# Gated DeltaNet block loop: other slots for a block's last pieces, another bank for the outputs, another way of the inverses to their rows

## The chip, the cores and the metric

The kernel runs on one core of one Trainium2 chip. The metric is the device time of one execution, in microseconds (us). The time of the kernel before is 2538.49 us, the median of three runs (2527.29 to 2549.32).

## The reference, cut to what matters

One inference step of a hybrid encoder layer: 4096 tokens of a prompt and 32 of a running stream, each token 1024 wide. Group A is a short gated convolution, group B a gated delta rule with 4 heads of 128. The change lies in group B and where group B meets group A.

```python
h    = rmsnorm(x, ln_pre);  proj = h @ w_in         # split into B_a C_a X_a Z_a | qkv | Z_g | decay, beta
y_a  = B_a * conv3(C_a * X_a) * silu(Z_a)           # group A
q, k, v = silu(conv4(qkv));  q, k = l2norm(q), l2norm(k)      # group B, per chunk of 64 tokens and head:
a_mat = tril(kbeta @ k^T * decay, -1)
t_mat = solve_triangular(I + a_mat, I)              # the inverses that the change carries in another way
u, w  = t_mat @ (v * beta), t_mat @ (kbeta * exp(g))
v_new = u - w @ S;  o = (q * exp(g)) @ S + (q @ k^T * decay) @ v_new
S     = S * exp(g_last) + k_dec^T @ v_new           # from chunk to chunk, 64 chunks in a row
y_g   = rmsnorm_head(o) * silu(Z_g)
y     = x + rmsnorm_post(concat(y_a, y_g) @ w_out)
```

In the kernel a chunk is 128 tokens (4 rows of 32 per inverse, merged to 128).

## The kernel before, in words

**Blocks and slots.** Group B goes over 16 prompt blocks of 256 tokens (two chunks each; the 32 sample tokens go along with block 0). A block runs eight pairs of projections (`steps`: k, k, q, q, v, v, z, z). A pair is two runs of 24 matmuls of 128x256 on TensorE (PE), and behind each run there is a *slot*: block gi has slots s0 = 16*gi to s0 + 15. What is not a projection is cut into pieces, which `at_slot` puts into a numbered slot and `run_slot` runs there. With `T.on` set, PE keeps exactly the order in which its matmuls are written; the other engines are ordered by a scheduler from what depends on what.

**A block's own pieces.** Slots s0 + 7 to s0 + 12: norms of q and k, Gram matrices (`gram`, tiles `gt`, `kd`, `at`), then `subst`. Slots s0 + 2 to 13 also hold the next block's gates and its normalized input. `subst` inverts 32x32 triangles by forward substitution on GpSimd (POOL): one scaling of `la` (L547, 128x1024), then 31 steps of two operations (L551, L552) on `lt`. In the kernel before, `lt` is stored in DRAM (L555, tile `ltd`) and read back by eight DMAs of 32-byte runs (L562) into `Tc`.

**A block's last pieces** run during the next block and a half (`finish`, slots from s0 + 22 on). `rec_a` of chunk c is four pieces: `rt` (transposed v); `rk`, `rq` (products with the state S); `rv` (inverse times right side, copied by ScalarE (ACT) to `vn`, L652); `rS` (new state, L659). `merge` is five pieces: it transposes `Tc` to `U` on VectorE (DVE, L583), and makes the 128x128 inverses from the 32x32 ones by small matmuls into a bank of PSUM called "m", with VectorE's `Rx` (L599) and ACT's copies to U (L605) between. `rec_b` is two pieces: `oo` (inner part of the output, bank "o", L670 ff.), then norms on VectorE and ACT (L682) and `om` (transposed output, bank "o" too), which VectorE multiplies into the gate `zg` (L688), and a DMA stores `zg` (L693). A bank that two pieces share makes the second wait until the first has been read.

**Queues.** All DMAs named here are issued by SyncE (SP) in order; they take eight counters in turn, so that one waits until the DMA eight before it has landed. Weight columns of group A are prepared during blocks 1 to 13 (`prep_a`; its first step on VectorE is L206, behind a load from DRAM); blocks 4, 7 and 10 begin two such columns.

**After block 15** the pieces that are left run one after the other with no projections between them; then group A begins (`operands`, `a_sample`, `a_pairs`), whose products are sums of 12 matmuls of 128x256 by a Strassen-Winograd scheme (`winograd`).

The pieces of a block's end stand in the code as:

```python
at_slot(s0 + 28, next, ra[1])        # rt of chunk 1
at_slot(s0 + 34, ends, rb[0])        # om of chunk 0
at_slot(s0 + 35, ends, ra[1])        # rS of chunk 1
at_slot(s0 + 35, next, rb[1])        # oo of chunk 1
at_slot(s0 + 39, ends, rb[1])        # om of chunk 1
```

Of the kernel before, what the change touches and what calls it, by code (L numbers as in the profile page):

```python
# [18 lines left out]
P = 128  # L19
# [30 lines left out]
def hybrid_kernel(  # L50
# [471 lines left out]
    def subst(b):  # L522
# [30 lines left out]
        b["subst_end"] = getattr(last, "ins", last)  # L553
        ltd = dp.tile([4, 32, 256], F32, tag="ltd", bufs=2, name=f"ltd{b['id']}")
# [13 lines left out]
    def merge(b):  # L568
# [11 lines left out]
        Tf = Tc.rearrange("p c h e -> p (c h) e")  # L580
        for q in range(nb):
            s = slice(32 * q, 32 * q + 32)
            V.transpose(Uf[s, :, s], Tf[s])  # L583
# [11 lines left out]
        for q in (0, 2):  # L595
            s0, s1 = slice(32 * q, 32 * q + 32), slice(32 * q + 32, 32 * q + 64)
            for c, h in ch:
                T.matmul(px[s1, c, h], M[c][s0, h, s1], Tc[s0, c, h], start=True, stop=True)
            V.tensor_tensor(X[s1], px[s1], bc(nb_[s1], 3, 32), ALU.mult)  # L599
# [63 lines left out]
    def rec_b(b, c):  # L663
# [5 lines left out]
        po = bank("o", [P, NH, P], f"o{nm}")[:C]  # L669
# [154 lines left out]
    def finish(p, s0):  # L824
# [5 lines left out]
        if n == 1:  # L830
            for i, g in enumerate((ra[0], ra[0], mg, ra[0], ra[0], rb[0])):
                at_slot(s0 + 16 + i, next, g, None)
            at_slot(s0 + 24, ends, rb[0])
            at_slot(s0 + 24, out_state, p)
            return
        at_slot(s0 + 22, next, ra[0])
        at_slot(s0 + 23, next, ra[0])
        for i in range(5):
            at_slot(s0 + 24 + i, next, mg, None)
        at_slot(s0 + 29, next, ra[0])  # L840
        at_slot(s0 + 30, ends, ra[0])
        at_slot(s0 + 30, next, rb[0])
        at_slot(s0 + 28, next, ra[1])
        at_slot(s0 + 32, next, ra[1])
        at_slot(s0 + 34, next, ra[1])
        at_slot(s0 + 34, ends, rb[0])
        at_slot(s0 + 35, ends, ra[1])
        at_slot(s0 + 35, next, rb[1])
        at_slot(s0 + 39, ends, rb[1])
        if p["last"]:  # L850
            at_slot(s0 + 36, out_state, p)
# [83 lines left out]
    T.on = False  # L935
    early.close()
    for i in sorted(slots):
        run_slot(i)
    late.close()
# [3 lines left out]
    pl2 = ctx.enter_context(tc.tile_pool(name="pl2", bufs=1, side="right", reuse_waits="tile"))  # L943
# [32 lines left out]
    def winograd(lts, rhs, ps, c11, c12, c21, c22):  # L976
# [4 lines left out]
        for i, p in enumerate(ps):  # L981
            mm3(p, lts[i], rhs[i], True, True)
            if i == 0:
# [154 lines left out]
    rm = t3([P, KT], F32, "rm")  # L1138

# [151 lines left out]
    a_pairs(1, ops[1], 0)  # L1291
    for i in range(4, 8):
# [67 lines left out]
```

## Time and profile before

| | us |
|---|---|
| median of three runs | 2538.49 |
| lowest, highest | 2527.29, 2549.32 |
| the profiled execution's own time | 2536.03 |
| its span | 2534.2 |
| blocks 1 to 14 and what is left of 0 (236.57 to 1413.73) | 1177.16 |
| PE, DVE, ACT, POOL busy in the whole span | 2178.5, 1697.0, 1003.4, 1168.1 |

The profile is one execution. Rows of a timeline read: start, duration, engine, line, operation, output tile <- input tiles, shape, how many in a row, and in brackets how long the engine had been idle before it and on what. PEclk is the granted TensorE clock as a share of 2.4 GHz; 0.50 is the lower level, 1.2 GHz. Tile names are those of the code without buffer numbers. An engine's idle time costs something only where another engine waits for it.

### The profile page before, as it was taken

The numbers are of one execution on the slowest core, as the hardware profiler recorded it, in microseconds if no ns is written. First come the engines' busy times: TensorE is split into PE (matmuls) and PEld (weight loads), VectorE is DVE, ScalarE is ACT, GpSimd is POOL, SyncE is SP. The second block draws the span as 40 slices with busy tenths as digits, with TensorE's granted clock in tenths as the row PEclk, the third lists the DMA queues.
The fourth block names the chain that finished last, engine by engine and source line by source line (L and its number), as shares of the span: only waits on it lengthen the run. The fifth ranks groups of instructions, "written<-read, shape, count | busy, mean of one in ns | idle before, by whom it ended". The sixth has DMA issues, their size and how long they took to land. (4 is left out here: it accounts for less than half of the span.)

```text
span 2534.2 us, 48623 instructions
## 1 busy us (share of the span) xinstructions
PE 2178.5 (86%) x18626; PEld 1745.3 (69%) x18626; DVE 1697.0 (67%) x4666; ACT 1003.4 (40%) x2497; POOL 1168.1 (46%) x1581
## 2 busy tenths in 40 slices
PE   4666988699878987888889879999999999999998
PEld 3555776577767776777777768878888888544443
DVE  4885767676777677767865667556667466576772
ACT  4453555355545554555554422112221111333331
POOL 3524532544454445344642464175665442265552
PEclk9777988898999888989989889999999999999999
DMA  6343323423332433234422331521212103344331
GB/s 117 53 106 78 80 60 72 89 69 101 80 90 63 108 79 90 62 102 86 92 55 52 114 104 27 202 76 49 77 51 75 51 30 134 111 146 153 115 128 67
DMA packets 296914, 221.40 MB, mean 87 GB/s; under 512 B 166392, under 2 KB 236856, under 8 KB 296680
## 3 DMA queue, kind: packets, MB, share of 16 engines
q1 hardware_dynamic: 296680, 218.28, 31.4%
q8 instruction: 146, 2.39, 0.4%
q14 instruction: 88, 0.72, 0.1%
HBM read 127.84 MB, written 74.64 MB: 80 GB/s over the span
## 5 line engine op out<-in xcount | busy, mean ns | idle before, releaser
L74 PEld LDWEIGHTS <-w 128*128 128x128 f16 x6528 | 640.8, 103 | 126.0 <-POOL w L714 24.2
L74 PE MATMUL pj_c<-hhi,w 128*128 128x256 f16 x3072 | 583.3, 290 | 0.0
L74 PE MATMUL pj_c<-hlo,w 128*128 128x256 f16 x1536 | 445.4, 290 | 0.0
L74 PEld LDWEIGHTS <-w_a 128*128 128x128 f16 x2880 | 272.1, 99 | 62.2 <-issue 26.5
L547 POOL TENSOR_TENSOR la<-la,lt 128x1024 f32<-128x1024 f32 x16 | 37.8, 2361 | 581.7 <-DVE lt L542 536.7
L74 PEld LDWEIGHTS <-opm 128*128 128x128 f16 x1536 | 149.1, 98 | 189.3 <-issue 13.8
L552 POOL TENSOR_TENSOR lt<-lt 128x112 f32<-128x112 f32 (+29 forms) x496 | 237.5, 479 | 38.7
L551 POOL TENSOR_TENSOR lt<-la,lt 128x112 f32<-128x112 f32 (+29 forms) x496 | 219.0, 442 | 38.9
L436 DVE SCALAR_TENSOR_TENSOR qk<-u,cw,qk 128x256 f32<-128x256 f32 x384 | 208.4, 587 | 4.8 <-ACT qk L434 4.8
L74 PE MATMUL pja<-op,w_a 128*128 128x256 f16 x1536 | 193.8, 276 | 6.7 <-ACT d L984 2.7
L74 PE MATMUL pj_z<-hhi,w 128*128 128x256 f16 x1024 | 180.3, 275 | 0.0
L74 PE MATMUL ga<-op,w_a 128*128 128x256 f16 x1152 | 152.2, 279 | 14.6 <-DVE w L988 7.0
L1186 POOL TENSOR_TENSOR mab<-mab 128x1024 bf16<-128x1024 bf16 (+2 forms) x48 | 103.6, 2158 | 128.1 <-ACT mab L1184 125.7
L74 PE MATMUL pj_z<-hlo,w 128*128 128x256 f16 x512 | 140.5, 274 | 0.0
L74 PE MATMUL pjo<-w_o,opm 128*128 128x512 f16 x528 | 118.2, 379 | 3.8 <-DVE v13y L1261 2.0
L74 PE MATMUL ro<-w_o,opm 128*128 128x512 f16 x504 | 113.1, 379 | 4.3 <-DVE v7y L1261 2.3
L988 DVE TENSOR_TENSOR w<-pja,w 128x256 f32<-128x256 f32 x168 | 67.3, 420 | 73.7 <-PE pja L74 70.6
L74 PE MATMUL go<-w_o,opm 128*128 128x512 f16 x504 | 112.7, 379 | 3.9 <-DVE v19y L1261 2.0
L1003 ACT ACTIVATE op<-tsc 128x512 f16<-128x512 f32 x60 | 37.8, 630 | 192.9 <-POOL tsc L1009 113.0
L468 ACT ACTIVATE jk<-gt 128x128 bf16<-128x128 f32 x256 | 71.0, 278 | 100.8 <-PE gt L77 95.2
L988 DVE TENSOR_TENSOR w<-ga,w 128x256 f32<-128x256 f32 x121 | 51.0, 422 | 77.6 <-PE ga L74 69.8
L436 DVE SCALAR_TENSOR_TENSOR v<-u,cw,v 128x256 f32<-128x256 f32 x192 | 84.6, 477 | 9.0 <-ACT v L434 9.0
(697 smaller groups left out, 4664.0 us busy)
## 6 DMA issues: line engine op xcount, KB each, us to landing
xt<-in_x_prompt_dram SPq DMA_DIRECT2D x32, 512.0 KB
op<-hTd SPq DMA_DIRECT2D x32, 512.0 KB
mx<-mxd SPq DMA_DIRECT2D x16, 1024.0 KB
xtw<-in_w_in_dram SPq DMA_DIRECT2D x28, 512.0 KB
wad<-hl SPq DMA_DIRECT2D x56, 256.0 KB
gB<-gd SPq DMA_DIRECT2D x16, 516.0 KB
hTd<-hhi SPq DMA_DIRECT2D x16, 512.0 KB
hTd<-hlo SPq DMA_DIRECT2D x16, 512.0 KB
```

Source lines behind the costliest of these rows:

```text
L74: return self.queue(nc.tensor.matmul(*a, **k))
L436: V.scalar_tensor_tensor(d, u[:, i, j:j + n], cw[:, j, c0 + i:c0 + i + 1], d, ALU.mult, ALU.add)
L468: A.activation(jk[:C], tp[:C, h, :], AF.Square, accum_out=b["ss"][:, c, x, h:h + 1])
L547: E.tensor_tensor(la, la, bc(rl, 1, 32), ALU.mult)
L551: E.tensor_tensor(tm, bc(la[:, j, j + 1:32], 2, w), bc(lt[:, j, 0:w], 1, r), ALU.mult)
L552: last = E.tensor_tensor(lt[:, j + 1:32, 0:w], lt[:, j + 1:32, 0:w], tm, ALU.subtract)
L988: V.tensor_tensor(dst, p, src, ALU.add)
L1003: A.activation(f[:, q, 0, hf], t, AF.Copy)
L1186: G.tensor_tensor(ab[:, 0:m], ab[:, 0:m], ab[:, m:2 * m], ALU.add)
```

## The change

1. **Inverses to rows.** `subst` no longer stores `lt` in DRAM. One VectorE transpose of 32x32 blocks writes `lt` into the first 256 columns of `la`, and 16 DMAs from SBUF to SBUF (32 rows of 256 bytes each) bring them to `Tc`, which now has the layout [P, 4, 2, NH, 8]. The transposes to U and the merge's first matmuls read that layout with another access pattern. The sample's path stays.
2. **Slots.** A block's last pieces start two slots later and end five slots later, with at most one piece of a chunk's chain in a slot in most places.
3. **Bank.** `rec_b`'s `po` goes to bank "m" (so its tile reads `mo` instead of `oo`).
4. **The end.** The pieces left after block 15 run between the products of group A's first two column blocks (`a_pairs(0, ., 0)` and `a_pairs(1, ., 0)`), behind each second product of `winograd`; the pools opened after them, and `operands(4)` to `(7)`, stand behind that.

```diff
--- before.py
+++ after.py
@@ -551,6 +551,16 @@
             E.tensor_tensor(tm, bc(la[:, j, j + 1:32], 2, w), bc(lt[:, j, 0:w], 1, r), ALU.mult)
             last = E.tensor_tensor(lt[:, j + 1:32, 0:w], lt[:, j + 1:32, 0:w], tm, ALU.subtract)
         b["subst_end"] = getattr(last, "ins", last)
+        if not b["s"]:
+
+            X = la.rearrange("p a b -> p (a b)")[:, 0:256].rearrange("p (q m e) -> p q m e", q=4, e=8)
+            V.transpose(X.rearrange("p q m e -> p e m q"), lt.rearrange("p a e -> p e a"))
+            Tc = b["Tc"] = tl([P, 4, 2, NH, 8], F32, "Tc", 1, b["id"])
+            for q in range(4):
+                for g in range(4):
+                    dma(Tc[32 * q:32 * q + 32, g].rearrange("p c h e -> p (c h e)"),
+                        X[32 * g:32 * g + 32, q].rearrange("p m e -> p (m e)"))
+            return
         ltd = dp.tile([4, 32, 256], F32, tag="ltd", bufs=2, name=f"ltd{b['id']}")
         dma(ltd.rearrange("g l f -> (g l) f"), lt.rearrange("p a b -> p (a b)"))
         tcl = te([P, 1, NH, 32], F32, "Tcs", 1, "s") if b["s"] else tl([P, 2, NH, 32], F32, "Tc", 1, b["id"])
@@ -577,10 +587,10 @@
         U = U2
         b["U"] = [U[:, c] for c in range(2)]
         Uf = U.rearrange("p c h e -> p (c h) e")
-        Tf = Tc.rearrange("p c h e -> p (c h) e")
+        Tf = Tc.rearrange("p g c h e -> p (c h) g e")
         for q in range(nb):
             s = slice(32 * q, 32 * q + 32)
-            V.transpose(Uf[s, :, s], Tf[s])
+            V.transpose(Uf[s, :, s].rearrange("p a (g e) -> p a g e", e=8), Tf[s])
         nm = b["id"]
         ch = [(c, h) for c in range(2) for h in range(NH)]
 
@@ -595,7 +605,8 @@
         for q in (0, 2):
             s0, s1 = slice(32 * q, 32 * q + 32), slice(32 * q + 32, 32 * q + 64)
             for c, h in ch:
-                T.matmul(px[s1, c, h], M[c][s0, h, s1], Tc[s0, c, h], start=True, stop=True)
+                T.matmul(px[s1, c, h].rearrange("p (g e) -> p g e", e=8), M[c][s0, h, s1], Tc[s0, :, c, h],
+                         start=True, stop=True)
             V.tensor_tensor(X[s1], px[s1], bc(nb_[s1], 3, 32), ALU.mult)
         yield
         for q in (0, 2):
@@ -666,7 +677,7 @@
         nm = f"{b['id']}_{c}"
         sl = slice(c * C, (c + 1) * C)
         o, vn = b["rec"].pop(c)
-        po = bank("o", [P, NH, P], f"o{nm}")[:C]
+        po = bank("m", [P, NH, P], f"o{nm}")[:C]
         for h in range(NH):
             T.matmul(po[:, h], b["at"][c][:, h, :C], vn[:, h], start=True, stop=True)
         V.tensor_tensor(o, o, po, ALU.add)
@@ -828,27 +839,17 @@
         rb = [rec_b(p, c) for c in range(n)]
         mg = merge(p)
         if n == 1:
-            for i, g in enumerate((ra[0], ra[0], mg, ra[0], ra[0], rb[0])):
-                at_slot(s0 + 16 + i, next, g, None)
-            at_slot(s0 + 24, ends, rb[0])
-            at_slot(s0 + 24, out_state, p)
+            for i, g in ((19, ra[0]), (20, ra[0]), (23, mg), (24, ra[0]), (25, ra[0]), (25, rb[0])):
+                at_slot(s0 + i, next, g, None)
+            at_slot(s0 + 30, ends, rb[0])
+            at_slot(s0 + 30, out_state, p)
             return
-        at_slot(s0 + 22, next, ra[0])
-        at_slot(s0 + 23, next, ra[0])
-        for i in range(5):
-            at_slot(s0 + 24 + i, next, mg, None)
-        at_slot(s0 + 29, next, ra[0])
-        at_slot(s0 + 30, ends, ra[0])
-        at_slot(s0 + 30, next, rb[0])
-        at_slot(s0 + 28, next, ra[1])
-        at_slot(s0 + 32, next, ra[1])
-        at_slot(s0 + 34, next, ra[1])
-        at_slot(s0 + 34, ends, rb[0])
-        at_slot(s0 + 35, ends, ra[1])
-        at_slot(s0 + 35, next, rb[1])
-        at_slot(s0 + 39, ends, rb[1])
+        for i, g in ((24, ra[0]), (25, ra[0]), (26, mg), (27, mg), (28, mg), (29, mg), (30, mg), (30, ra[1]),
+                     (31, ra[0]), (33, ra[0]), (33, rb[0]), (35, ra[1]), (37, ra[1]), (38, rb[0]),
+                     (39, ra[1]), (39, rb[1]), (44, rb[1])):
+            at_slot(s0 + i, next, g, None)
         if p["last"]:
-            at_slot(s0 + 36, out_state, p)
+            at_slot(s0 + 40, out_state, p)
 
     def first_group(grp):
 
@@ -932,15 +933,11 @@
             if b["last"]:
                 out_hist(b)
         prevs = grp
-    T.on = False
     early.close()
-    for i in sorted(slots):
-        run_slot(i)
-    late.close()
 
 
     pe2 = ctx.enter_context(tc.tile_pool(name="pe2", bufs=1, side="left", reuse_waits="tile"))
-    pl2 = ctx.enter_context(tc.tile_pool(name="pl2", bufs=1, side="right", reuse_waits="tile"))
+    pl2 = None
 
     def t2(shape, dtype, tag, bufs=1, nm=""):
         return pe2.tile(shape, dtype, tag=tag, bufs=bufs, name=f"{tag}{nm}")
@@ -980,6 +977,8 @@
 
         for i, p in enumerate(ps):
             mm3(p, lts[i], rhs[i], True, True)
+            if i % 2 and slots:
+                run_slot(min(slots))
             if i == 0:
                 A.activation(c21, p, AF.Copy)
             else:
@@ -1135,8 +1134,6 @@
         V.tensor_copy(hr, hp)
         dma(dst[0, 0].rearrange("j (c p) -> (j c) p", p=P), hr)
 
-    rm = t3([P, KT], F32, "rm")
-
     def prep_out(i):
 
         w = t3([P, 2, D], F32, "mx", 2, f"w{i}")
@@ -1289,6 +1286,12 @@
     a_sample(0)
     a_pairs(0, ops[0], 0)
     a_pairs(1, ops[1], 0)
+    while slots:
+        run_slot(min(slots))
+    T.on = False
+    late.close()
+    pl2 = ctx.enter_context(tc.tile_pool(name="pl2", bufs=1, side="right", reuse_waits="tile"))
+    rm = t3([P, KT], F32, "rm")
     for i in range(4, 8):
         operands(i)
     a_pairs(0, ops[0], 1)
```

**PE, last pieces of block 6, which run in block 7.** In a row stand the line, the operation, output <- inputs, shape; `pj_c` is a projection, `rv_1`, `rS_1` and `oo_1` belong to chunk 1, `om_0` to chunk 0. Before, ahead of the run of 24 projections between `rv` and `rS`:

```order
L74 MATMUL pj_c_10863<-hhi_9848,w_22_507 128x256
L74 MATMUL rv_1_10888<-R_1_10476,U 128x128 x4
L77 MATMUL om_0_10895<-ident,o_0_10109 128x128 x4
L74 LDWEIGHTS w_23_510
L74 MATMUL pj_c_10863<-hhi_9848,w_23_510 128x256
```

and behind that run of 24:

```order
L74 MATMUL pj_c_10863<-hhi_9848,w_23_511 128x256
L74 MATMUL rS_1_10972<-vn_1_10893,kd_1_9149 128x128 x4
L74 MATMUL oo_1_10982<-vn_1_10893,at_1_9424 128x128 x4
L74 LDWEIGHTS w_16_681
L74 MATMUL pj_c_11008<-hhi_9848,w_16_681 128x256
```

Now `rv` stands two runs of 24 ahead of `rS`, and `om_0` one run ahead of it. The end of the second run and what follows:

```order
L74 MATMUL pj_c_11090<-hhi_9871,w_18_857 128x256
L77 MATMUL om_0_11115<-ident,o_0_10276 128x128 x4
L74 LDWEIGHTS w_19_860
L74 MATMUL pj_c_11090<-hhi_9871,w_19_860 128x256
```

```order
L74 MATMUL pj_c_11090<-hhi_9871,w_19_861 128x256
L74 MATMUL rS_1_11159<-vn_1_11088,kd_1_9148 128x128 x4
L74 MATMUL mo_1_11169<-vn_1_11088,at_1_9445 128x128 x4
L77 MATMUL gt_0_11196<-ident,qk_10803 128x128 x4
L74 LDWEIGHTS w_24_1208
```

What moved: a whole run of projections lies between `rv` and `om_0` and another between `om_0` and `rS`; `rS` and the output product still stand side by side, but the latter is in the merge's bank.

**VectorE in block 7, around the second q pair** (`u_2`, `qk`: that pair's convolution; `o`, `so`, `S`: last pieces of the block before). Before:

```order
L688 SCALAR_TENSOR_TENSOR zg_7586<-om_1_10088,gwc,zg_7586 128x4x128
L431 COPY hist_9725<-u_2_10075 128x6
L436 SCALAR_TENSOR_TENSOR qk_9722<-u_2_10075,cw,qk_9722 128x256
L639 SCALAR_TENSOR_TENSOR R_0_10046<-rk_0_10095,sm_9453,R_0_10046 128x128 x4
L436 SCALAR_TENSOR_TENSOR qk_9722<-u_2_10075,cw,qk_9722 128x256 x5
L471 TENSOR_TENSOR kd_0_10124<-gt_0_10115,E_9602 128x512
L429 COPY u_10_10389<-hist_8640 128x2x3
L583 STREAM_TRANSPOSE U<-Tc_9538 32x8x32 x4
L599 TENSOR_TENSOR Rx_10187<-m_10188,sm_9453 32x256 x2
```

Now:

```order
L699 SCALAR_TENSOR_TENSOR zg_7592<-om_0_10054,gwc,zg_7592 128x4x128
L557 STREAM_TRANSPOSE la_9480<-lt_9481 128x8x8x4
L431 COPY hist_9745<-u_2_10085 128x6
L670 SCALAR_TENSOR_TENSOR S_1_10103<-S_0_9815,E_7484,rS_1_10098 128x128 x4
L436 SCALAR_TENSOR_TENSOR qk_9742<-u_2_10085,cw,qk_9742 128x256 x2
L683 TENSOR_TENSOR o_1_9955<-o_1_9955,mo_1_10108 128x512
L436 SCALAR_TENSOR_TENSOR qk_9742<-u_2_10085,cw,qk_9742 128x256 x2
L471 TENSOR_TENSOR kd_0_10144<-gt_0_10135,E_9632 128x512
L593 STREAM_TRANSPOSE U<-Tc_9558 32x8x32
L436 SCALAR_TENSOR_TENSOR qk_9742<-u_2_10085,cw,qk_9742 128x256 x2
L689 TENSOR_TENSOR so_1_10114<-so_1_10114,sm_8382 128x4
```

What moved: a new transpose out of `lt` stands right ahead of the q pair's copy, and the four transposes to U no longer stand together; the other three follow 6, 17 and 27 rows behind the first. Counted one by one, 11, 17, 28 and 41 instructions stand between the new transpose and the four.

**SP in block 7, around the DMAs of the inverses.** Before, and now:

```order
L555 DMA ltd_9536<-lt_9460 128x256
L736 DMA wad_122<-hl_0_10126 128x1024
L562 DMA Tc_9538<-ltd_9536 128x4x8 x8
L693 DMA mxd_112<-zg_7586 128x4x128
L736 DMA wad_122<-hl_1_10130 128x1024
```

```order
L299 DMA hTd_104<-hlo_9872 256x1x1024
L704 DMA mxd_112<-zg_7592 128x4x128
L561 DMA Tc_9558<-la_9480 32x64 x16
L747 DMA wad_122<-hl_0_10146 128x1024
L747 DMA wad_122<-hl_1_10150 128x1024
```

Nine DMAs of a block, one behind the other through DRAM, have become 16 that wait for VectorE's transpose and for no other DMA's data.

## Rows read from the trace of the kernel before

**Rows 1.** Stretches: us, busy of PE PEld DVE ACT POOL (x), PEclk, DMA share, GB/s.

```profile
236.57:1413.73 1177.16, 1005.98 (x9221) 872.79 (x9220) 842.95 (x2614) 626.72 (x1660) 532.09 (x1011) 0.91 0.32 80
...
925.20:965.80 40.60, 37.77 (x388) 32.81 (x387) 26.10 (x95) 21.59 (x64) 0.04 (x1) 0.96 0.13 26
```

**Rows 2.** What PE waited for, whole span: us in total, times, longest us.

```profile
PE om L77 <- DVE o L682: 49.1, 7, 17.6
PE oo L74 <- DVE zg L688: 44.0, 13, 4.6
PE m L74 <- DVE Rx L599: 33.9, 15, 5.5
...
PE m L74 <- DMA Tc<-ltd: 20.5, 17, 7.4
PE rS L74 <- ACT vn L652: 20.1, 13, 2.3
```

**Rows 3.** Timeline of PE, end of block 6's chunk 1.

```profile
894.73 1.11 PE L74 MATMUL rv<-R,U 128*128 128x128 f32 x8
...
901.35 2.08 PE L74 MATMUL rS<-vn,kd 128*128 128x128 f32 x8 [2.28 <-ACT vn L652]
907.26 2.07 PE L74 MATMUL oo<-vn,at 128*128 128x128 f32 x8 [3.83 <-DVE zg L688]
```

**Rows 4.** Stretches around these two waits, columns as in group 1.

```profile
901.40:907.00 5.60, 2.03 (x8) 1.73 (x8) 5.60 (x6) 3.61 (x5) 5.13 (x7) 0.50 0.90 198
907.00:909.50 2.50, 2.24 (x10) 2.11 (x11) 2.50 (x10) 0.67 (x2) 2.19 (x5) 0.50 0.70 110
909.50:913.00 3.50, 3.50 (x25) 2.74 (x23) 2.04 (x5) 1.28 (x8) 2.87 (x9) 0.72 0.70 67
```

**Rows 5.** Line L547 and timeline of POOL: first and last instruction of block 7's pass, next pass.

```profile
L547 POOL TENSOR_TENSOR la<-la,lt x16: 2352/2360/2375, 184.8 to 1470.7; 128x1024 f32<-128x1024 f32 x16
...
883.61 2.35 POOL L547 TENSOR_TENSOR la<-la,lt 128x1024 f32<-128x1024 f32 x1 [28.87 <-DVE lt L542]
...
919.67 0.20 POOL L552 TENSOR_TENSOR lt<-lt 128x8 f32<-128x8 f32 x1
...
965.76 2.36 POOL L547 TENSOR_TENSOR la<-la,lt 128x1024 f32<-128x1024 f32 x1 [42.20 <-DVE lt L542]
```

**Rows 6.** Timeline of DVE: the second q pair's copy between these passes.

```profile
925.19 0.16 DVE L431 COPY hist<-u 128x6 f32<-128x6 f32 x1
```

**Rows 7.** Timelines of SP and PE: the inverses' DMAs in two blocks, and their reader.

```profile
488.30 2.13 SPq L555 DMA_DIRECT2D ltd<-lt  x1
...
499.78 4.22 SPq L562 DMA_DIRECT2D Tc<-ltd  x8
...
583.08 4.34 SPq L562 DMA_DIRECT2D Tc<-ltd  x8
...
589.55 0.40 PE L74 MATMUL m<-Tc,M 32*32 32x32 f32 x4 [0.84 <-DMA Tc<-ltd]
```

**Rows 8.** Groups by line and form, VectorE's transposes: busy us, mean ns | idle before.

```profile
L583 DVE STREAM_TRANSPOSE U<-Tc 32x256 f32<-32x256 f32 x64 | 27.8, 435 | 12.1 <-DMA Tc<-ltd 11.1 <-issue 0.2
```

**Rows 9.** Timelines: DVE's L206 in block 4; PE's longest waits, blocks 1, 4, 7, 10.

```profile
489.55 1.22 DVE L206 TENSOR_TENSOR xtw<-xtw,lnp 128x1024 f32<-128x1024 f32 x1 [8.73 <-DMA xtw<-in_w_in_dram]
...
222.34 1.91 PE L74 MATMUL rvs<-Rs,Uss 32*32 32x128 f32 x8 [23.33 <-DVE Uss L574]
...
504.90 1.08 PE L77 MATMUL om<-ident,o 128*128 128x128 f32 x4 [17.59 <-DVE o L682]
...
761.51 1.09 PE L77 MATMUL om<-ident,o 128*128 128x128 f32 x4 [11.77 <-DVE o L682]
...
1014.22 1.09 PE L77 MATMUL om<-ident,o 128*128 128x128 f32 x4 [11.69 <-DVE o L682]
```

**Rows 10.** PE's wait for Tc between 1413.73 and 1597.64 (us, times, longest), and that stretch.

```profile
PE m L74 <- DMA Tc<-ltd: 15.1, 6, 7.4
...
1413.73:1597.64 183.91, 155.53 (x1509) 133.18 (x1508) 117.78 (x314) 48.72 (x154) 84.18 (x125) 0.91 0.30 94
```

## Prediction

> **What bounds the kernel now.** I read the stretches first. Between 236.57 and 1413.73 us lie 14 blocks, 84.1 us each; PE is busy 1005.98 of 1177.16 us, DVE 842.95, POOL 532.09 [rows 1]. So PE bounds the block loop, and what is not PE work in it is 171 us of PE standing still, plus a granted clock of 0.91. The list of what PE waited for tells why it stands [rows 2]: for the output product's bank (oo behind zg, 44.0 us), for the merge's Rx (33.9), for ACT's vn (20.1), for the inverses' DMAs (20.5), and for an o that VectorE brings late (49.1).
>
> The first and third of these are one place, seen in the timeline of PE [rows 3]. rv ends at about 895.8, om of chunk 0 follows it, 24 projections run (about 2.7 us), then rS waits 2.28 us for vn and oo 3.83 us for the product of zg, which must read om's bank before oo may write it. The stretches there show a second price [rows 4]: PE works at 0.50 of the clock (1.2 GHz) from 901.40 to 909.50 and at 0.72 until 913.0. It did 2.03 + 2.24 us of work at half speed, which would have taken half, and 3.50 us at 0.72 of speed: 2.1 + 1.0 = 3.1 us. I take 2.5 a block, since not each block has the full drop.
>
> Four long waits are of another kind [rows 9]: 23.33, 17.59, 11.77 and 11.69 us, together 64.4, in blocks 1, 4, 7 and 10, where VectorE stands in L206 behind a load (8.73 us in block 4) and what PE needs is queued behind it.
>
> Last I looked for what else goes round with the block, on POOL [rows 5]: 15 periods between the first and last L547, (1470.7 - 184.8) / 15 = 85.7 us. Less the four long waits it is (1285.9 - 64.4) / 15 = 81.4 us. One pass takes 919.87 - 883.61 = 36.3 us, and POOL then idles for most of the rest. VectorE does not wait for POOL before: its copy for the second q pair stands at 925.19 [rows 6], 5.3 us after the pass's end.
>
> **The change part by part.** *Bank and slots.* In the merge's bank the output product no longer waits for zg, and with 24 projections between rv and om and 24 more before rS, vn is ready (it was 2.28 us late, one run of 24 lasts some 2.7). That removes 44.0 + 20.1 us [rows 2] and the clock's 2.5 x 13 = 32. The shorter om waits, 49.1 - 41.05 = 8, go too. Of the waits for Rx I take half, 17, since the slots still follow each other run by run; the bounds are 0 and 33.9. The new bank can make a merge wait for o's reading; they lie slots apart (output pieces at 33 and 39, the merge at 26 to 30 of the next or same block), so I cost it at nothing; if that cover is gone it costs at most what the old bank did, 3.4 us a block.
>
> *Inverses to rows.* Before, eight DMAs issue in 4.34 us (0.54 each), and the reader starts at 589.55, 2.13 us after the last issue [rows 7]. Of the waits for Tc, 15.1 us lie after 1413.73 [rows 10], so 5.4 lie in the loop; these go. New is a transpose of 128x256. Not in the trace; by the nearest row, 435 ns for 32x256 [rows 8], and VectorE works on partitions side by side, so 0.44, or twice that with the scattered pattern; 0.6 us. It adds 10 us of VectorE's time in all, and VectorE has 24 us a block free [rows 1]. The DMAs grow from 9 to 16. At 0.54 each and 2.13 for landing, the four groups are there 4.3, 6.4, 8.6 and 10.8 us after the transpose. VectorE reaches the four transposes to U after 11, 17, 28 and 41 instructions. In 925.20 to 965.80 it did 95 instructions, 26.10 us busy [rows 1]: 0.27 us each if it never idles, 0.43 with its idling. So it comes to them after 3.0, 4.7, 7.7, 11.3 us at the earliest, 4.7, 7.3, 12, 17.6 at the latter pace. The first stalls are between 0 and 1.7 us; I take 0.5 a block.
>
> The Trainium skill speaks against this part: "DMA: Bandwidth & Descriptors", section "Rules for kernel authors", says to coalesce many small transfers into one, as under 64 KB one pays mostly overhead, and the section on the anatomy of one DMA gives about 2.0 us fixed for each. By that, an estimate of 16 x 2.0 = 32 us if each were paid in turn; the trace does not agree for the old eight, whose issue took 4.34 us together.
>
> *Where the wait comes back.* The new transpose waits for POOL's last step, and in VectorE's order it stands right ahead of the second q pair's copy. Behind that copy are the q pair's convolutions, the norms, the Gram matrices, and with them the next block's L542 that starts POOL. So the pass and this chain can no longer overlap: they form a ring. Its length: pass 36.3, transpose 0.6, then from the copy to the next L547 965.76 - 925.19 = 40.6, in which PE was busy 37.77 us [rows 1], so little can be saved; I take 1.5 us off for Rx and the smaller waits, add 0.5 for the first stalls, and get 76.4, say 76. The removed waits alone would give less: 44.0 + 20.1 + 32 + 8 + 17 + 5.4 = 126.5 us over the loop, 8.4 a block, 81.4 - 8.4 = 73. So the ring takes 3 us a block of it back, and PE will stand where VectorE is late with the copy behind POOL.
>
> *The four long waits.* L206 stays, and the o that is queued behind it too; the later slots give some room. I take 40%: 26 of 64.4 us; bounds 0 and all.
>
> *The end.* Between 1413.73 and 1597.64 PE stands 28.4 us, 15.1 for Tc [rows 10]. The last pieces now have products beside them. But block 15's inverses still come after POOL's last pass, and products were already free to run while pieces waited, since the strict order was off there. I take a third of 15.1, 5; bounds 0 and 15.
>
> *Sum,* against the profiled execution's own 2536.03 (2.5 below the median of 2538.49): (81.4 - 76) x 15 = 81 from the loop, 26, 5: 112. 2536 - 112 = 2424, rounded 2425.
>
> **The rivals.** *The ring doesn't bind.* The copy's slack of 5.3 us [rows 5, 6] speaks for it: if POOL starts earlier in its block than I think, all of 126.5 is kept, with half of the long waits (32) and 5 to 8 of the end: 165, 2371. Against it: the ring's 76 is above 73.
>
> *Half comes back.* VectorE, with 60.2 us of work a block, stands for POOL and for the DMAs, and PE for it, so the block takes 79 instead of 76: (81.4 - 79) x 15 = 36, a quarter of the long waits (16), nothing at the end: 52, 2484. For it: VectorE's order is strict, a late Tc stops everything behind it. Against: the landing times above. At its end, with 80.5 a block, it gives 13 + 10: within 1%.
>
> *Slower: the DMAs of the inverses land late.* One place: the last transpose to U. Under other traffic the store of lt and the reading back lay 11.5 us apart (488.30 to 499.78) [rows 7], for what is 2.1 us otherwise. Were the 16 DMAs, eight at a time by their counters, to take two such times and 2 more, the last is there after 25 us; VectorE comes to it after 14.4 (mean of 11.3 and 17.6) and stands 10.6 us in each block: period 76 + 10.6 = 86.6, (86.6 - 81.4) x 15 = 78 more, less 26: 2588. It decides from the point where the stall eats the gain: 81.4 + 31 / 15 - 76 = 7.5 us a block, which is a landing 22 us after the transpose. Against it: the DMA share there is 0.13 [rows 1], the long spread stood in a block with weight loads, and runs of 256 bytes replace runs of 32.
>
> **How the numbers follow.** The ring 0.50 (2405 to 2450), it doesn't bind 0.20 (2360 to 2400), half comes back 0.24, of which 0.06 within 1%, late DMAs 0.06. A measurement of this kernel can tell about 1%, so faster is below 2513, slower above 2564. Faster: 0.50 + 0.20 + 0.18 = 0.88; same 0.06; slower 0.06. The range takes in the first two and the third's middle: 2365 to 2495.
>
> **What would show it.** In the list of PE's waits oo behind zg and rS behind vn must be gone (each under 5 us), and the clock about 0.95 in the loop. POOL's L547 starts must lie 76 us apart in blocks without two weight columns. VectorE must show waits for POOL at the new transpose, 2 to 4 us in most blocks; if it shows none, the first rival holds. Waits of VectorE at its transposes to U above 2 us a block speak for the second, above 7.5 for the third. If waits for Rx stay at 34 us, that term was wrong; if the stretch after the last block is no shorter, so was the end's. The forecast is wrong as a whole if what PE waits for merely changes its name and the period stays above 80.

## The result and the profile after

The changed kernel takes 2560.88 us (median of six runs, 2557.54 to 2565.92) against 2537.63 us of the kernel before beside it: ratio 1.0094, 95% interval 1.0065 to 1.0123. It is slower by 0.9%, where 4.4% faster was forecast. The profiled execution has a span of 2558.4 us (before 2534.2).

The list of what PE waited for, whole span of the changed kernel (total, times, longest), answers to [rows 2]:

```profile
PE om L77 <- DVE o L693: 106.2, 14, 18.3
PE m L74 <- DVE Rx L610: 75.5, 16, 9.5
...
PE ga L74 <- DVE w L987: 20.2, 10, 9.0
PE rq L74 <- ACT R L643: 12.4, 6, 2.5
...
PE rS L74 <- ACT vn L663: 7.5, 8, 1.5
```

The waits that the change was aimed at are gone: oo behind zg (44.0) has left the list, vn fell from 20.1 to 7.5 and the inverses' DMAs (20.5) are not in it. In their place om waits 106.2 us for o (49.1 before) and the merge 75.5 us for Rx (33.9).

The block loop, and the stretch from POOL's last L547 to the first product of group A with operand 4 (columns as in [rows 1]); the first row answers to [rows 1], the POOL line to [rows 5]:

```profile
236.57:1413.73 1177.16, 965.93 (x9044) 840.76 (x9043) 844.84 (x2579) 607.97 (x1618) 548.63 (x1017) 0.91 0.31 79
1463.30:1625.23 161.93, 113.96 (x1123) 95.93 (x1120) 98.70 (x241) 30.72 (x91) 73.48 (x95) 0.89 0.18 60
```

```profile
L547 POOL TENSOR_TENSOR la<-la,lt x16: 2349/2355/2361, 184.9 to 1463.3; 128x1024 f32<-128x1024 f32 x16
```

The same stretch of the kernel before:

```profile
1470.70:1597.64 126.94, 109.94 (x1100) 94.09 (x1099) 92.24 (x236) 29.46 (x90) 74.58 (x95) 0.92 0.28 91
```

This is the whole account. From the first to the last L547 the loop takes 1278.4 us instead of 1285.9: 7.5 us less. The end stretch takes 161.93 instead of 126.94: 35.0 us more, with 4 us more of PE work and 31 us more of PE standing (48.0 against 17.0). What follows is 3.4 us shorter. The last L547 starts 7.4 us earlier, and -7.4 + 35.0 - 3.4 = 24.2 us, the difference of the spans. So there are two questions: why the end lost 35 us, and why the loop gained 7.5 where 107 were forecast.

### The profile page after: what moved, and what is told of

Its sections match the earlier page's. It is cut to its first block, busy times and chain, and to the rows that moved or that the text cites. A ratio compares the mean times of both kernels' runs of the same rounds, so it can differ in the third digit from the quotient of the medians.

```text
span 2558.4 us, 48870 instructions
## 1 busy us (share of the span) xinstructions
PE 2152.1 (84%) x18626; PEld 1725.5 (67%) x18626; DVE 1717.0 (67%) x4682; ACT 996.2 (39%) x2497; POOL 1183.9 (46%) x1581
## 5 line engine op out<-in xcount | busy, mean ns | idle before, releaser
L74 PE MATMUL pj_c<-hhi,w 128*128 128x256 f16 x3072 | 577.4, 288 | 0.0
L547 POOL TENSOR_TENSOR la<-la,lt 128x1024 f32<-128x1024 f32 x16 | 37.7, 2356 | 564.9 <-DVE lt L542 564.9
L552 POOL TENSOR_TENSOR lt<-lt 128x112 f32<-128x112 f32 (+29 forms) x496 | 241.1, 486 | 38.8
L551 POOL TENSOR_TENSOR lt<-la,lt 128x112 f32<-128x112 f32 (+29 forms) x496 | 223.9, 451 | 38.8
L77 PE MATMUL om<-ident,o 128*128 128x128 f32 x128 | 23.2, 311 | 106.2 <-DVE o L693 106.2
L436 DVE SCALAR_TENSOR_TENSOR v<-u,cw,v 128x256 f32<-128x256 f32 x192 | 97.3, 530 | 8.8 <-ACT v L434 8.4
```

Source lines behind the costliest of these rows:

```text
L74: return self.queue(nc.tensor.matmul(*a, **k))
L77: return self.queue(nc.tensor.transpose(*a, **k))
L436: V.scalar_tensor_tensor(d, u[:, i, j:j + n], cw[:, j, c0 + i:c0 + i + 1], d, ALU.mult, ALU.add)
L547: E.tensor_tensor(la, la, bc(rl, 1, 32), ALU.mult)
L551: E.tensor_tensor(tm, bc(la[:, j, j + 1:32], 2, w), bc(lt[:, j, 0:w], 1, r), ALU.mult)
L552: last = E.tensor_tensor(lt[:, j + 1:32, 0:w], lt[:, j + 1:32, 0:w], tm, ALU.subtract)
```

## The experiments

Ratios are to the kernel before, timed beside each on the same chip.

### The end

**The loop's changes with the old end.** The end's edits undone (order lifted and pieces run in a row after block 15):

```
-    while slots:  run_slot(min(slots))      # after a_pairs(1, ., 0)
+    T.on = False                            # ahead of early.close(), as before
+    for i in sorted(slots):  run_slot(i)
```

> The changed kernel with the end of the kernel before: after block 15 the strict order of PE is lifted, the pools are opened, and only then the 20 last pieces are written. Theory A (the strict order of PE at the end holds group A's first products back: from the last POOL pass to the first product of operand 4 it took 127 us before and 162 us after, while the block loop gained 7 us): about 2530 us, the stretch back at 127 us. Rival (the end is longer because the last block's pieces come later by their slots, or their inverses do): about 2560 us, the stretch stays at 155 us or more.

2523.34 us, ratio 0.9937 (0.9910 to 0.9964). Theory A held: the end stretch is 127.6 us again.

**The end alone** in the kernel before, the same edits the other way.

> The kernel before with the change's end alone (last pieces between the products of group A's first two column blocks under PE's strict order). Theory A: 2538 + 28 to 35 = about 2568 us, with waits of half a microsecond between a product and the next, and a wait for the merge's VectorE step of some 8 us. Rival (the end costs only with the later slots): about 2538 us.

2570.60 us, ratio 1.0134 (1.0105 to 1.0163): the end costs 30 us by itself. In it and in the changed kernel the products stand like this (timeline of PE, changed kernel):

```profile
1517.70 1.47 PE L74 MATMUL pja<-op,w_a 128*128 128x256 f16 x12 [0.47 <-ACT w L983]
...
1521.43 1.47 PE L74 MATMUL ga<-op,w_a 128*128 128x256 f16 x12 [0.51 <-DVE d L987]
...
1526.84 1.47 PE L74 MATMUL pja<-op,w_a 128*128 128x256 f16 x12 [0.85 <-DVE w L987]
...
1545.39 2.72 PE L74 MATMUL ga<-op,w_a 128*128 128x256 f16 x12 [8.98 <-DVE w L987]
```

Every second or third product waits half a microsecond or more for the reader of its bank, and one waits 8.98 us and then runs at the lower clock (granted 0.53 from 1545.30 to 1548.20, and 2.72 instead of 1.47 us). Summed over 1470 to 1630 us, PE's waits for such readers are 25.5 us here and 3.0 in the kernel before; its waits for operands are 15.7 and 4.5.

**The new end without the strict order.** One line in the changed kernel:

```
+    T.on = False
     early.close()
```

> The changed kernel with one edit: PE's strict order is lifted after block 15, ahead of group A's first products; the last pieces are still written between these products, and the pools and operands 4 to 7 still come after them. Theory A (the strict order is what costs the end some 37 us): about 2525 us, close to the 2523 us of the run with the old end. Rival A2 (it is the loads of operands 4 to 7, issued some 31 us later than before, or the later pools): 2550 us or more.

2527.98 us, ratio 0.9945 (0.9923 to 0.9967). Theory A held. So it is the order, not the place of the pieces or of the later loads: with PE free to take what is ready, the end stretch of the new end is 131.0 us (1459.70 to 1590.66), 4 us from the old one.

### The loop: one part at a time

**Slots and bank without the new way of the inverses** (the three hunks in `subst` and `merge` undone, old end).

> The kernel before with the later slots and the outputs in the merge's bank, the inverses still through DRAM, the end as before. Theory B (VectorE's new place for the inverses, behind POOL and with its four transposes to U far apart, is what brings the merge's waits for Rx from 34 to 75 us): those waits fall back to 34 us, the waits for the bank (44 us) and for vn stay gone: about 2490 us. Rival C (the later slots themselves are at fault: output pieces land behind the weight columns' loads on VectorE, and the merge's first piece behind a busy VectorE): 2525 to 2540 us, waits for o still about 100 us.

2517.97 us, ratio 0.9917 (0.9887 to 0.9947). Theory B fell: waits for o are 109.2 us and for Rx 70.9 us without VectorE's new place too. They come with the slots or the bank; the bank alone, below, tells the two apart.

**The inverses' new way alone.**

> The kernel before with the new way of the inverses to their rows alone (VectorE's transpose and 16 DMAs from SBUF to SBUF). Theory B: waits for Rx grow by some 40 us, the waits for the inverses' DMAs (20 us) go: about 2555 us. Rival C: the way through SBUF is a small gain, about 2525 us.

2533.45 us, ratio 0.9982 (0.9963 to 1.0001): nothing that can be told apart. Rx waits fell (19.2 us), waits for the inverses rose (30.8).

**The bank alone.**

```
-        po = bank("o", [P, NH, P], f"o{nm}")[:C]
+        po = bank("m", [P, NH, P], f"o{nm}")[:C]
```

> The kernel before with the output product in the merge's bank alone. Theory C (the bank is the useful part, and the later slots give its gain back): the 44 us of waits for the bank go and most of the half clock behind them with them, 2538 - 44 - 25 = about 2470 us. Rival D (the bank's wait only stands in for VectorE being late in that stretch, so that PE then waits for the next thing VectorE brings): 2515 to 2530 us, with new waits of some 3 us behind the same place.

2548.26 us, ratio 1.0032 (1.0008 to 1.0055). The 44 us of waits are gone, and nothing is gained: waits for o rise from 49.1 to 106.5 us, those for the inverses' DMAs to 36.0. Theory C fell, and the time lies above rival D's 2515 to 2530 us as well. Waits for Rx stay at 33.5 us: so the bank is enough to bring the waits for o, and those for Rx come with the later slots. The slots without the bank were not run.

**Bank and inverses** together.

> The kernel before with the merge's bank and the inverses through SBUF, slots and end as before. Theory C: both gains add, some 5 to 7 us under the bank alone, about 2465 us. Rival D: as the bank alone or slower, 2515 to 2535 us, since VectorE's new wait for POOL falls on an engine that is late.

2533.39 us, ratio 0.9965 (0.9947 to 0.9983); waits for o 107.3 us. Rival D held: the two gains do not add up to 2465 us.

**Less work for VectorE.** The last tap of the q and k convolutions is left out (the result is then another one), in the kernel before and in the bank alone:

```
-            for j in range(1, 4):
+            for j in range(1, 4 if c0 >= 8 else 3):
```

> The kernel before without the last tap of the q and k convolutions on VectorE (it leaves out 128 of 384 such operations, 8 a block, some 0.55 us each: 4.4 us a block, 70 us in all). Theory D (VectorE paces the first two thirds of a block, and PE's waits are where its lag shows): 40 to 60 us faster, about 2490 us. Rival E (PE waits for where the pieces stand and for loads, not for the amount of VectorE's work): less than 20 us, above 2520 us.

> The merge's bank for the outputs alone, with the same work left out (8 operations of the q and k convolutions a block). Theory D: with VectorE lighter the bank's wait is worth something: 15 to 30 us under the kernel before with the same work left out, about 2465 us. Rival E: 5 us over it, as without the cut, about 2520 us, waits for o still at some 100 us.

2546.38 us (ratio 1.0028, 1.0008 to 1.0049) and 2557.39 us (1.0067, 1.0045 to 1.0089). VectorE had 68 us less of this work (256 instead of 384 operations, 140.3 instead of 208.4 us), and neither kernel became faster. In the lightened kernel before even the wait of oo behind zg fell to 4.2 us, while that for vn rose from 20.1 to 45.1. So the amount of this work is not the bound, and theory D fell in that form.

**Chunk 0's output later.**

```
-  (38, rb[0]), (39, ra[1]), (39, rb[1]), (44, rb[1])
+               (39, ra[1]), (39, rb[1]), (41, rb[0]), (44, rb[1])
```

> The run with later slots and the merge's bank (2518 us), with chunk 0's transposed output three slots later (41 instead of 38). Theory C1 (109 us of waits for o come from the place of om alone: the o is brought late, and 8 us of cover ends the wait): waits for o below 40 us, about 2465 us. Rival D (VectorE is the engine that bounds these slots, and what PE waits for only changes its name): waits for Rx or other VectorE products grow by what those for o lose, 2500 to 2520 us.

2507.26 us, ratio 0.9860 (0.9838 to 0.9882). The waits for o (109 us) are gone, but those for Rx rose from 71 to 89, for vn to 39 and for R to 27 us: of 109 us some 11 were won. Theory C1 fell (2465 us), rival D held.

**The weight columns' code later** (`if si == 3:` to `if si == 4:`).

> The run with later slots and the merge's bank (2518 us), with the weight columns' preparation begun one pair (two slots) later in the block, so that VectorE's wait for their loads (50 us in all) stands behind chunk 0's output instead of ahead of it. Theory C3 (the eight long waits for o, 10 to 19 us each, are the weight columns' work ahead of o in VectorE's queue): waits for o below 40 us, about 2465 us. Rival D (VectorE is full there in any order): about 2510 us, other waits longer in the same blocks.

2522.35 us, ratio 0.9915 (0.9895 to 0.9935). This settles nothing: the loads and L206 were issued at the same moments as before (second L206 of block 6 at 635.28 against 636.05), since VectorE's order comes from what depends on what, not from where the code stands.

### The queue in front of o

In the timelines of VectorE and PE of the changed kernel, block 6:

```profile
639.09 1.23 DVE L206 TENSOR_TENSOR xtw<-xtw,lnp 128x1024 f32<-128x1024 f32 x1 [4.12 <-DMA xtw<-in_w_in_dram]
...
647.89 0.69 DVE L693 TENSOR_TENSOR o<-o,so 128x512 f32<-128x512 f32 x1
```

```profile
648.64 1.11 PE L77 MATMUL om<-ident,o 128*128 128x128 f32 x4 [11.53 <-DVE o L693]
```

VectorE stands 4.12 us for a weight load; o is scaled behind it and behind what piled up meanwhile, and PE waits 11.53 us. Before, the blocks 3, 6, 9 and 12 paid 1.6 to 2.5 us at this place and 4, 7 and 10 11.7 to 17.6 [rows 9]; now these seven blocks pay 10.6 to 18.3. With the bank alone the same seven pay 8.6 to 24.3 already.

**L206 on POOL**, with slots and bank:

```
-            (V if ct in VLN or not first else G).tensor_tensor(w, w, bc(lnp, 2, n), ALU.mult)
+            (V if ct in VLN else G).tensor_tensor(w, w, bc(lnp, 2, n), ALU.mult)
```

> The run with later slots and the merge's bank (2518 us) with the weight columns' first operation (scaling behind their load, two in each of eight blocks) on POOL instead of VectorE. Theory C3 (VectorE's 50 us of standing for these loads, ahead of o in its queue, make the eight long waits for o): those waits fall from 109 to below 50 us, about 2475 us. Rival D (VectorE is late there by its work): waits for o stay above 80 us, about 2510 us.

2488.79 us, ratio 0.9795 (0.9744 to 0.9846). Theory C3 held in its waits: 25.6 us for o instead of 109.2, and 29 us won at once (some 43 were expected).

**The same by order alone**: L206 stays on VectorE, queued behind the scaling of chunk 0's o.

```
-  with tc.issue_after(p["subst_end"]):
+  with tc.issue_after(p["subst_end"]), tc.issue_after(scaling of o, two blocks back):
```

> The later slots and the merge's bank (2518 us), with the weight columns' VectorE operations queued behind the scaling of chunk 0's o (order only). Theory F: as with these operations on POOL, waits for o below 40 us, about 2490 us; the wait for the loads then falls on R and Rx behind it, some 10 us of it. Rival D: above 2510 us.

2503.69 us, ratio 0.9867 (0.9849 to 0.9885). Waits for o 24.3 us: it is the queue's order. The stand for the loads now falls partly on Rx (98.3 us), and the time is 14 us above theory F's 2490.

**Order alone with the bank alone**, behind chunk 1's o:

> The merge's bank for the outputs alone (2548 us), with the weight columns' VectorE operations queued behind the scaling of chunk 1's o (order only; nothing else is moved by hand). Theory F (the o stands behind VectorE's wait for the weight loads in an in-order queue, and this alone eats the bank's gain): waits for o fall from 107 to below 40 us, about 2490 us. Rival D (VectorE is late there anyway): above 2530 us, waits for o still above 80 us.

2543.74 us, ratio 1.0024 (1.0011 to 1.0038). Half of theory F held, its price did not. Two lists of PE's waits, first of this run, then of the next one:

```profile
PE m L74 <- DMA Tc<-ltd: 89.1, 102, 13.9
PE m L74 <- DVE Rx L599: 46.1, 15, 5.3
...
PE om L77 <- DVE o L682: 16.8, 9, 2.1
```

```profile
PE m L74 <- DMA Tc<-ltd: 51.0, 68, 8.9
PE m L74 <- DVE Rx L599: 41.1, 15, 5.0
PE oo L74 <- DVE zg L688: 38.8, 13, 3.4
```

Of the 90 us that o gave back, 53 are now waited for the inverses' DMAs (89.1 instead of 36.0) and 13 for Rx.

**L206 on POOL in the kernel before, nothing else.**

> The kernel before with the weight columns' first operation on POOL instead of VectorE, nothing else. Theory J (the waits stand one behind the other; with slots and bank of before, the wait for o goes and the bank's 44 us and the inverses' DMAs are met instead): about 2525 us, so that the change's loop parts are worth some 40 us on top of it (2484 us with all). Rival (the loads alone were the loss): 2495 us or less.

2546.44 us, ratio 1.0034 (1.0016 to 1.0053). The edit that wins 29 us with the later slots wins nothing without them. The waits did what theory J says (oo 38.8 us, DMAs 51.0), but the time is 21 us above its 2525, and no run shows why.

### The ring that was there before

Why nothing helps in the old slots is seen on POOL, VectorE and PE. A regular block (5) of the kernel before, then of the run with bank and order:

```profile
546.43 2.36 POOL L547 TENSOR_TENSOR la<-la,lt 128x1024 f32<-128x1024 f32 x1 [28.33 <-DVE lt L542]
...
584.09 1.11 DVE L431 COPY hist<-u 128x6 f32<-128x6 f32 x1
...
594.31 1.05 PE L74 MATMUL m<-Tc,M 32*32 32x32 f32 x16 [4.37 <-DVE Rx L599]
...
630.47 2.36 POOL L547 TENSOR_TENSOR la<-la,lt 128x1024 f32<-128x1024 f32 x1 [30.70 <-DVE lt L542]
```

```profile
547.95 2.36 POOL L547 TENSOR_TENSOR la<-la,lt 128x1024 f32<-128x1024 f32 x1 [32.78 <-DVE lt L542]
...
591.71 0.31 PE L74 MATMUL m<-Tc,M 32*32 32x32 f32 x2 [1.36 <-DMA Tc<-ltd]
...
630.89 2.36 POOL L547 TENSOR_TENSOR la<-la,lt 128x1024 f32<-128x1024 f32 x1 [30.56 <-DVE lt L542]
```

Before: from the start of the pass to the merge's last inverse 589.55 - 546.43 = 43.1 us (34.9 of POOL and 8.2 for two trips of DMA, [rows 7]), from there over the merge, the Gram matrices and L542 to the next pass 40.9 us. With bank and order the two are 43.8 and 39.2. The merge stands in PE's strict order ahead of the same block's Gram matrices, so pass, DMAs, merge, Gram matrices and the next pass are a ring. The waits for oo, vn and o lie in its first leg, beside POOL's pass; those for Rx lie in the second.

Two legs make up a period wherever one cuts it; whether the ring sets the period is told by what is waited for where they join. In block 5 before, PE waited there 0.84 us for the DMAs, and then 4.37 us for Rx, which came at the end of a queue of VectorE without a gap. So another path was the longer one, by about 1 us: with bank and order the period of this block fell only from 84.04 to 82.94 us.

Over the whole loop the same is found by following each wait back to what ended it, from the last L547 to the first. This chain runs through POOL's pass in 5 of the 15 periods of the kernel before, and through a weight load of 9 to 19 us in six. With bank and order it runs through the pass in 12 of 15. So the ring stood right behind the other waits, and it set the period as soon as they were gone. No run shortened POOL's pass, so this is read from traces and not shown by an edit.

### The later slots, and what is left

What the later slots are worth is seen between the two runs by order alone. With the old ones the merge's first products wait 89.1 us for the inverses' DMAs, with the later ones 11.8, and the mean period falls from 85.6 to 82.9 us: 41 us over the loop.

**Slots, bank, inverses and L206 on POOL** (the changed kernel with the old end and that one line):

> The changed kernel with the end of before, and the weight columns' first operation on POOL instead of VectorE: slots, bank and the inverses through SBUF together. Theory G (the inverses' new way exchanges VectorE's stand for the DMAs, 45 us, for a stand for POOL of about 30 us, and is worth little): within 8 us of the 2489 us of the same without it. Rival (it was hidden behind the loads): 2475 us or less.

2484.45 us, ratio 0.9790 (0.9765 to 0.9815), 4 us from the same without the inverses' new way: theory G. VectorE's stand for the DMAs (44.9 us) is gone, and it stands for POOL in every block instead:

```profile
DVE la L557 <- POOL lt L552: 62.7, 15, 6.3
```

This is the ring of the prediction: VectorE waits for POOL at the new transpose in 15 blocks, and the chain of waits runs through the pass in 13 of 15 periods. But its second leg is longer than forecast: from the new transpose to the next L547 it takes 44.7 to 49.6 us in the blocks that begin one weight column, where 0.6 + 39.1 + 0.5 = 40.2 was forecast.

**Without POOL's weight work**, with slots, bank and L206 on POOL. Subtractions of the lower halves and sums of quarters left out (the result is then another one):

```
-            G.tensor_tensor(hl[:, 1], src, hl[:, 0], ALU.subtract)
+            A.activation(hl[:, 1], src, AF.Copy)
-        G.tensor_tensor(a22, a21, a22, ALU.add)      # and three more
```

> The run with slots, bank and the weight columns' first operation on POOL (2489 us), with POOL's work on the second half of each weight column left out (it leaves out the lower halves' subtractions and the sums of quarters, 11 operations of 128x512 in each of 13 blocks; the lower halves are copies by ACT). Theory H (VectorE's small operations take 1.1 us instead of 0.17 while POOL does these, the output's chain of them stands ahead of Rx, and so Rx is late): waits for Rx fall from 85 to below 50 us, about 2455 us. Rival I (Rx is late by its place behind R and the v convolutions): waits for Rx stay above 70 us, 2480 us or more.

2460.62 us, ratio 0.9690 (0.9666 to 0.9714), 28 us less than with them. Waits for Rx are 69.1 us: of 85 us 16 come from POOL's neighbourhood, so neither H nor I held as put.

**The merge one slot later**, on top of all of the loop:

```
-  (26, mg) ... (30, mg), (30, ra[1]), (31, ra[0]), (33, ra[0]), (33, rb[0]), ... (38, rb[0])
+  (27, mg) ... (31, mg), (31, ra[1]), (32, ra[0]), (34, ra[0]), (34, rb[0]), ... (40, rb[0])
```

> All of the change's loop parts, the old end and the weight columns' first operation on POOL (2484 us), with the merge's five pieces and rv one slot later (27 to 31 and 32; rS and the output of chunk 0 in 34, chunk 1 as it was). Theory K (Rx is late against PE by a fixed stretch of VectorE's queue, so one run of 24 projections more covers some 2.8 us in each of 15 blocks): waits for Rx from 93 to about 55 us, about 2455 us, with some 10 us of new waits for S. Rival (VectorE sets the pace there, the wait keeps its length or moves to rv or rS): 2475 to 2490 us.

2477.78 us, ratio 0.9758 (0.9735 to 0.9781): the fastest kernel here that computes everything, 60 us under the kernel before and 83 under the changed one. But waits for Rx only fell from 92.9 to 84.3 us, with 26.4 us new for `kd`. Theory K fell and its rival held: Rx is not late by a fixed stretch. The place in VectorE's queue in front of it, in the changed kernel's block 11:

```profile
1099.59 1.23 DVE L689 TENSOR_TENSOR so<-so,sm 128x4 f32<-128x4 f32 x1
...
1101.06 1.12 DVE L134 TENSOR_SCALAR so<-so 128x4 int32<-128x4 int32 x1
...
1105.35 1.12 DVE L650 SCALAR_TENSOR_TENSOR R<-rk,sm,R 128x128 f32<-128x128 f32 x4
...
1110.66 0.44 DVE L593 STREAM_TRANSPOSE U<-Tc 32x256 f32<-32x256 f32 x1
...
1111.62 0.68 DVE L693 TENSOR_TENSOR o<-o,so 128x512 f32<-128x512 f32 x1
...
1112.82 0.42 DVE L610 TENSOR_TENSOR Rx<-m,sm 32x256 f32<-32x256 f32 x1
```

```profile
1103.08 0.69 PE L74 MATMUL m<-Tc,M 32*32 32x32 f32 x16
1113.29 1.05 PE L74 MATMUL m<-Tc,M 32*32 32x32 f32 x16 [9.53 <-DVE Rx L610]
```

The whole norm of chunk 1's output (`so`, o) and the fourth transpose to U stand ahead of Rx, though its product was there at 1103.8. With the old slots that norm lay in an earlier stretch. What share of the wait is this order and what the rest was not separated, since no run moved Rx alone: it stays open.

## Why the prediction was wrong, point by point

- **The removal of the old waits** was right, item by item: oo gone, vn from 20.1 to 7.5, the inverses' DMAs gone, VectorE's wait for POOL at the new transpose 29.9 us in 9 blocks (3.3 each, forecast 2 to 4), its waits at the transposes to U 9.9 us in all. The new transpose took 0.68 us (0.6 taken), the 16 DMAs issued in 10.8 us in block 11 (8.6 taken) and landed in time. The rival of late DMAs did not come true. The fixed cost of 2.0 us that the prediction takes from the Trainium skill, "DMA: Bandwidth & Descriptors", stands there in the section on the path of DMAs that GpSimd issues; these 16 were issued by SyncE.
- **The failed step in the loop is the ring's length of 76 us**, and in it the second leg, 40.6 us less 1.5. It was read in one block, in which the copy comes 5.3 us after the pass and the leg is short. In block 5 of the same trace the copy stands at 584.09, 2.8 us after the pass, and the next L547 at 630.47: 46.4 us. With that leg the ring is 34.9 + 0.6 + 46.4 = 81.9 us (an estimate from these rows), no less than the 81.4 it was to improve on. In the changed kernel the leg, from the new transpose to the next L547, was forecast at 40.2 us and took 46.6 to 48.7 in all nine blocks from 2 to 13 that begin one weight column. Here are two of them, 6 and 11 (columns as in [rows 1]):

```profile
650.45:697.24 46.79, 44.30 (x432) 37.56 (x431) 31.43 (x116) 24.84 (x78) 0.74 (x5) 0.93 0.12 30
1091.23:1139.77 48.54, 36.01 (x368) 30.74 (x366) 35.17 (x108) 22.57 (x68) 14.21 (x17) 0.89 0.20 61
```

  In blocks 3, 6, 9 and 12 PE hardly waits in it (2.2 to 4.1 us), but more matmuls fall into it, 432 against the 388 of [rows 1] in block 6. In blocks 2, 5, 8, 11 and 13 PE stands 10 to 12.5 us, 7.1 to 9.5 of them for Rx. The period of L547 was 85.2 us in the mean, 1278.4 / 15. And the ring was not new: it lay right behind the other waits in the old slots already, through the merge.
- **The sum of waits** ("126.5 us over the loop, 8.4 a block"), which gave the prediction its lower bound of 73 us, failed too. It took each wait as time that leaves with its cause. The bank's 44 us, taken away alone, made the time 0.3% longer. Behind them stood the next in line: o behind L206 in VectorE's queue, then the inverses behind POOL and two DMAs, each shown by the run that removed the one ahead of it.
- **The term for Rx** was forecast to halve (17 us off); it rose from 33.9 to 75.5 us, with the later slots. They put the output's norm ahead of Rx, which was in plain sight in the order of VectorE's instructions shown with the change: a row of `so` stands between the transposes to U. How much of the rise is due to it stays open.
- **The long waits**: 26 of 64.4 us were to go. That of block 1 (23.33 us) did; those behind L206 spread from three blocks to seven, 106.2 us for o instead of 49.1. The line of the prediction that the later slots "give some room" did not come true: chunk 0's output still stood behind the loads. But the slots are not the cause, since the bank alone gives the same seven blocks. Nor was a long wait worth its length before: the periods of blocks 1, 4, 7 and 10 are 5.9 to 11.8 us above the mean of the others (83.3 us), for waits of 11.69 to 23.33.
- **The end** is the second failed step: it was taken as 5 us won, and it lost 35. The text names the reason that decides, "products were already free to run while pieces waited, since the strict order was off there", and put what keeping the order on costs at nothing. Lifting the order gave 33 us back.
- **The clock**: 0.91 in the loop as before, 0.95 forecast, since PE stands as long in other places.
- The rival "half comes back" came nearest in its mechanism (VectorE stands for POOL and PE for VectorE), but almost all came back (7.5 us of 107 stayed), and none of the rivals had the end. The text's own last test came true: what PE waits for changed its name and the period stayed above 80.
- Slips in names, without weight in the sum: the pieces that run in block 7 under the names of "block 6" are those of block 5, since a block's last pieces run up to two blocks later. The rows from 883.61 to 965.80 are of block 9, not 7. The stretch from 236.57 to 1413.73 begins inside block 1 and ends inside block 15.

## What to carry to other kernels

A list of waits is no list of savings: before adding waits up, close the ring that sets the period (here POOL's pass, the DMAs, the merge, the Gram matrices, POOL again) and ask which wait stands behind each one that is taken away. Measure a leg of such a ring in several blocks, not in one. An in-order queue that stands for a load holds up everything queued behind it: moving one such instruction to another engine won 29 us with the later slots and the bank, and nothing without them. A strict order of the matmuls cost 33 us at the end of this kernel, where short products wait for their banks: there, letting the engine take what is ready gave them back.

## What the runs showed of the hardware

VectorE's small operations slow down beside POOL's large ones. In the fence above a 128x4 operation takes 1.23 and 1.12 us; POOL ran these in the same moments:

```profile
1099.34 1.46 POOL L756 TENSOR_TENSOR xtw<-xtw,xtw 128x512 f32<-128x512 f32 x1
1100.88 1.27 POOL L758 TENSOR_TENSOR xtw<-xtw 128x512 f32<-128x512 f32 x1
```

Both ended within 0.03 us of POOL's operation. In the kernel before, the first of the two (its line there is L678) took 0.17 us in the median of 32, here 0.42. Of the 448 operations of 128x4 that write `so`, 26 took over 0.6 us in the changed kernel and 5 in the kernel before, and each of these ended within 0.1 us of the end of an operation of POOL. All 448 together took 115 us instead of 105. With L206 on POOL they took 148, and 104 without POOL's weight work, a run that was 28 us faster; how much of that is due to these operations was not separated. The Trainium skill, "SBUF — State Buffer", section "SBUF: two separate sides", says that VectorE and GpSimd share one pair of ports as an exclusive lock: a GpSimd instruction and a VectorE instruction that is in a two-port mode, or has two inputs in SBUF (this only beside a GpSimd instruction that reads SBUF), shut each other out for the whole instruction. These ends agree with that.
